# Low parts of stored weights made by an accumulating transfer instead of a VectorE subtraction

## The chip, the cores and the metric

The kernel runs on one core of a Trainium2 chip. The metric is the time of one execution on the device in microseconds (us); the kernel before was timed three times, and beside these stands one profiled execution whose trace is read below. A few names: TensorE (PE in the profile) multiplies matrices, and PEld is its loading of weights; VectorE (DVE), ScalarE (ACT) and GpSimd (POOL) are the other engines; SyncE (SP) issues transfers (DMA). SPq and POOLq are the queues from which SP and POOL issue them.

## The reference, cut to what matters

The reference is one step of a decoder trunk of two layers over 1,024 prompt positions and 8 sample positions (model width 1,024), in float32:

```
p = x @ w_in                        # layer 0: 3072 columns (HGRN2 recurrence + Conformer convolution), layer 1: 3 * 1024 (short conv)
m = mixer(p) @ w_out                # recurrence, depthwise convolution, gates in between
x = layernorm(ALPHA * x + m)
x = layernorm(ALPHA * x + (silu(x @ w1) * (x @ w3)) @ w2)     # hidden width 2816, in both layers
```

What matters here is that every `@` above multiplies by a weight matrix that lies in HBM (memory), and that the results are wanted at nearly float32 precision.

## The kernel before, in words

All activations are kept transposed: 128 features on the partitions, positions along the row. The 1,032 positions form three chunks, `CH`: 0 and 1 of 384 columns and 2 of 264 columns.

**High and low parts.** TensorE multiplies in fp32r, a format with fewer bits than float32. Each operand is therefore split: the high part is the operand rounded to fp32r (`SC.copy`, the CAST on ScalarE at L120), the low part is the operand minus its high part (`VE.tensor_tensor(..., ALU.subtract)` on VectorE at L121). A product takes three matmuls for each 128 rows of weights: low weight by high activation, high by low, high by high (L141, L142, L143). The first of the three needs the weight's low part.

**Units.** A unit is a block of 1,024 x 128 weights (`load_unit`): SP loads 512 KB to a buffer `raw` (R_BUFS = 4 of them), ScalarE makes `wh` of it, VectorE makes `wl` of `raw` and `wh`. `wh` and `wl` have W_BUFS = 3 buffers each, so the split of unit j + 3 can begin only when TensorE has finished with unit j. `mm` runs a unit against one chunk: 8 x 3 matmuls of 384 or 264 columns. In `down` (products by w2) one unit holds several shorter blocks, but again 1,024 x 128 weights in all; sixteen units of `ffn_down` hold half as many.

**Seven products.** `main_g` runs most of the channel mixer for chunks 0 and 1 by a scheme of seven products for a 2 x 2 block product. `project` takes two units of w1 or w3 (`a`, `b`), makes four tiles of split weights and runs seven products of 12 matmuls on them: A11 and A12 (parts of the first unit as it lies in memory), S2 and S3, S4 and S1 (sums and differences of weights, which VectorE forms in `sa` and `sb` first), and A22 (half of the second unit as it lies in memory). Between the w1 and the w3 projection of a pair of blocks stands one `down` of the pair before, two units.

**Order.** The program is written once; a scheduler fixes the order of instructions on each engine when it is built, and every engine then runs its own list in order, waiting on semaphores. The stages on TensorE, in order of time: layer 0's mixer with its convolution interleaved with the first part of its channel mixer (to about 520 us), the rest of its mixer and the head of the channel mixer (to 925), the seven products (to 1163), the 264-column chunk and the norms (to 1259); then layer 1 likewise (mixer to 1532, head to 1785, seven products to 2203, the 264-column chunk and the last norms to the end). In the 264-column stages a unit is used for one chunk only.

Of the kernel before, what the change touches and what calls it, by code (L numbers as in the profile page):

```python
# [19 lines left out]
AF = mybir.ActivationFunctionType  # L20
ALU = mybir.AluOpType
PSUM = bass.MemoryType.PSUM

P = 128
# [5 lines left out]
NK = D // P  # L30
# [38 lines left out]
def trunk(ctx: ExitStack, tc: tile.TileContext, xT, win0, wout0, win1, wout1, w1, w3, w2, vecs, sh, scf, ssc,  # L69
          masks, eye, yT, hp, cp_o, sp_o, hs, cs_o, ss_o):  # L70
    nc = tc.nc
    VE, SC, GP, PE = nc.vector, nc.scalar, nc.gpsimd, nc.tensor
# [46 lines left out]
    def split(hi, lo, src):  # L119
        SC.copy(hi, src)  # L120
        VE.tensor_tensor(lo, src, hi.bitcast(F32), ALU.subtract)  # L121

    def load_unit(src, kt, n=NK):

        wh = wsp.tile([P, NK, P], F32R, name="wh")
        wl = wsp.tile([P, NK, P], F32R, name="wl")
        raw = wsp.tile([P, NK * P], F32, name="raw", bufs=R_BUFS).rearrange("p (k f) -> p k f", f=P)
        src = src.rearrange("p (k f) -> p k f", f=P)
        for k in range(0, kt, n):
            e = min(k + n, kt)  # L130
            nc.sync.dma_start(raw[:, k:e], src[:, k:e])
            split(wh[:, k:e], wl[:, k:e], raw[:, k:e])
        return wh, wl, kt

    def mm(unit, c, parts=None):

        wh, wl, kt = unit
        ps = mmp.tile([P, 512], F32, name="mm")[:, :CH[c][1] - CH[c][0]]
        for k in range(kt):
            h, l = (parts or xp)(k, c)  # L140
            PE.matmul(ps, wl[:, k, :], h, start=k == 0, stop=False)  # L141
            PE.matmul(ps, wh[:, k, :], l, start=False, stop=False)  # L142
            PE.matmul(ps, wh[:, k, :], h, start=False, stop=k == kt - 1)  # L143
        return ps
# [7 lines left out]
    first_x = load_x(0, 2)  # L152
    next(first_x)
    first_unit = [load_unit(win0[4], NK, 4)]
    for _ in first_x:
        pass
# [104 lines left out]
    def residual(m, c, ps, first):  # L261
        v = rc[c][:, m, :]
        if first:
            VE.scalar_tensor_tensor(v, v, ALPHA, ps, ALU.mult, ALU.add)
        else:
            VE.tensor_tensor(v, v, ps, ALU.add)  # L266

    def out_proj(wsrc, chunks):

        for m in range(NK):  # L270
            u = load_unit(wsrc[m], NK)
            for c in chunks:
                residual(m, c, mm(u, c), True)

    def ffn_up(tile_of, l, m, chunks, put, table=True):

        sl = {}
        u = load_unit(w1[l, m], NK)
        for c in chunks:
            s = tile_of(CH[c][1] - CH[c][0])  # L280
            ps = mm(u, c)
            if table:
                SC.activation(s, ps, AF.Silu)
            else:
                SC.activation(s, ps, AF.Sigmoid)
                VE.tensor_tensor(s, ps, s, ALU.mult)
            sl[c] = s
        u = load_unit(w3[l, m], NK)
        for c in chunks:
            s = sl[c]  # L290
            VE.tensor_tensor(s, mm(u, c), s, ALU.mult)
            split(*put(m, c), s)
# [299 lines left out]
    class Swiglu:  # L592
# [10 lines left out]
        def down(self, ms, chunks, first=()):  # L603

            n = len(ms)
            q = NK // n
            for m0 in range(0, NK, q):
                raw = wsp.tile([P, NK * P], F32, name="raw", bufs=R_BUFS).rearrange("p (k f) -> p k f", f=P)
                wh = wsp.tile([P, NK, P], F32R, name="wh")
                wl = wsp.tile([P, NK, P], F32R, name="wl")  # L610
                src = w2[self.l, m0:m0 + q][:, :, ms[0] * P:(ms[0] + n) * P].rearrange("q p f -> p q f")
                nc.sync.dma_start(raw.rearrange("p (q n) f -> p q (n f)", q=q), src)
                split(wh, wl, raw)
                for j in range(q):
                    u = wh[:, j * n:(j + 1) * n], wl[:, j * n:(j + 1) * n], n
                    for c in chunks:
                        residual(m0 + j, c, mm(u, c, lambda k, c: self.parts[ms[k], c]), c in first)
# [53 lines left out]
        def project(self, src, m, out, done):  # L671

            raws = []
            for w in (src[self.l, m], src[self.l, m + 1], None, None):
                r = wsp.tile([P, NK * P], F32, name="raw", bufs=R_BUFS).rearrange("p (k f) -> p k f", f=P)
                if w is not None:
                    nc.sync.dma_start(r, w.rearrange("p (k f) -> p k f", f=P))
                raws.append(r)
            a, b, sa, sb = raws
            lo, hi = slice(0, 4), slice(4, 8)  # L680

            def parts(r, n=NK):
                wh = wsp.tile([P, NK, P], F32R, name="wh")
                wl = wsp.tile([P, NK, P], F32R, name="wl")
                split(wh[:, :n], wl[:, :n], r)
                return [(wh[:, s], wl[:, s]) for s in (lo, hi)]

            def product(w, t):
                ps = mmp.tile([P, 512], F32, name="mm")[:, :384]
                for k in range(4):  # L690
                    PE.matmul(ps, w[1][:, k], t[0][:, k], start=k == 0, stop=False)  # L691
                    PE.matmul(ps, w[0][:, k], t[1][:, k], start=False, stop=False)  # L692
                    PE.matmul(ps, w[0][:, k], t[0][:, k], start=False, stop=k == 3)  # L693
                return ps

            def put(i, c, x, y, op):
                o = out(i, c)
                VE.tensor_tensor(o, x, y, op)
                done(i, c, o)

            A11, A12 = parts(a)
            u, v = self.short(), self.short()
            p1 = product(A11, (X0HA, X0LA))
            SC.copy(u, p1)
            p2 = product(A12, (X0HB, X0LB))
            put(0, 0, u, p2, ALU.add)
            VE.tensor_tensor(sa[:, hi], a[:, lo], b[:, lo], ALU.add)
            VE.tensor_tensor(sa[:, lo], sa[:, hi], b[:, hi], ALU.add)
            S2, S3 = parts(sa)
            p6 = product(S2, self.T2)  # L710
            VE.tensor_tensor(u, u, p6, ALU.add)
            p7 = product(S3, self.T3)
            VE.tensor_tensor(v, p7, u, ALU.subtract)
            VE.tensor_tensor(sb[:, lo], sa[:, lo], a[:, hi], ALU.add)
            VE.tensor_tensor(sb[:, hi], b[:, lo], b[:, hi], ALU.add)
            S4, S1 = parts(sb)
            p3 = product(S4, (X1HB, X1LB))
            VE.tensor_tensor(u, u, p3, ALU.add)
            p5 = product(S1, (X1HA, X1LA))
            put(1, 1, v, p5, ALU.subtract)  # L720
            put(0, 1, u, p5, ALU.add)
            A22, _ = parts(b[:, hi], 4)
            p4 = product(A22, self.T4)
            put(1, 0, v, p4, ALU.add)

# [39 lines left out]
    with tc.tile_pool(name="t0", bufs=1, reuse_waits="tile") as tp:  # L765
        F0.T2, F0.T3 = t_pair(tp, 2), t_pair(tp, 3)
        with tc.tile_pool(name="head0", bufs=1, reuse_waits="tile") as act:
# [6 lines left out]
            for m in range(0, NEARLY, 4):  # L774
# [4 lines left out]
                p = tc.cur_priority  # L779
                F0.down(ms, (1, 2))  # L780
        with tc.tile_pool(name="main0", bufs=1, reuse_waits="tile") as act:
            F0.T4 = t_pair(act, 4)
            F0.main_pool(act)
            q = tc.cur_priority
# [71 lines left out]
    with tc.tile_pool(name="t1", bufs=1, reuse_waits="tile") as tp:  # L856
        F1.T2, F1.T3 = t_pair(tp, 2), t_pair(tp, 3)
        with tc.tile_pool(name="head1", bufs=1, reuse_waits="tile") as act:
# [10 lines left out]
            p = tc.cur_priority  # L869
            F1.down(ms, ALL, ALL)  # L870
        with tc.tile_pool(name="main1", bufs=1, reuse_waits="tile") as act:
            F1.T4 = t_pair(act, 4)
            F1.main_pool(act)
            q = tc.cur_priority
# [74 lines left out]
```

## Time and profile before

| What | Value |
|---|---|
| Time, median of three runs | 2383.87 us (2382.72 to 2384.26) |
| Profiled execution, its own time | 2385.06 us |
| Span of the trace | 2383.2 us |
| Mean granted clock of TensorE | 0.989 of full speed |
| PE busy | 2333.2 us, 98% of the span |
| DVE busy | 1701.4 us, 71% |
| ACT busy | 874.2 us, 37% |
| POOL busy | 45.3 us, 2% |
| Transfers | 229.79 MB, mean 96 GB/s |

Busy time is time in which an engine has at least one instruction under way. The trace's span begins a little after the timed execution does and ends before it, so the profiled time is 1.9 us longer than the span. A busy share near 100% says that an engine is never without work, not that it works at its peak.

### The profile page before, as it was taken

The numbers are of one execution on the slowest core, as the hardware profiler recorded it, in microseconds if no ns is written. First come the engines' busy times: TensorE is split into PE (matmuls) and PEld (weight loads), VectorE is DVE, ScalarE is ACT, GpSimd is POOL, SyncE is SP. The second block draws the span as 40 slices with busy tenths as digits, with TensorE's granted clock in tenths as the row PEclk, the third lists the DMA queues.
The fourth block names the chain that finished last, engine by engine and source line by source line (L and its number), as shares of the span: only waits on it lengthen the run. The fifth ranks groups of instructions, "written<-read, shape, count | busy, mean of one in ns | idle before, by whom it ended". The sixth has DMA issues, their size and how long they took to land.

```text
span 2383.2 us, 36586 instructions
## 1 busy us (share of the span) xinstructions
PE 2333.2 (98%) x14974; PEld 2293.0 (96%) x14974; DVE 1701.4 (71%) x2943; ACT 874.2 (37%) x1479; POOL 45.3 (2%) x40
## 2 busy tenths in 40 slices
PE   9999999999899999999998999999999999999997
PEld 8999899999899999999998999999999999999997
DVE  8998789897863336777686423667957777777775
ACT  5434353335631223332354211435513332332553
POOL 0000000000000000000000000000000000000000
PEclk9999999999999999999999999999999999999998
DMA  5322222453341221222342311334402222132663
GB/s 186 116 78 73 88 78 77 123 167 113 116 131 45 79 73 48 68 80 71 119 149 88 90 53 45 90 115 142 133 27 71 63 80 68 57 89 80 194 196 98
DMA packets 85560, 229.79 MB, mean 96 GB/s; under 512 B 8225, under 2 KB 26401, under 8 KB 85137
## 3 DMA queue, kind: packets, MB, share of 16 engines
q1 hardware_dynamic: 85232, 227.02, 30.9%
q8 instruction: 117, 1.92, 0.3%
q0 software_dynamic: 160, 0.45, 0.1%
q14 instruction: 51, 0.41, 0.1%
HBM read 220.22 MB, written 7.21 MB: 95 GB/s over the span
## 4 chain that ended last, share of the span: by engine, by line
PE 91%; DVE 4%; ACT 2%; POOL 1%; DMA 1%; issue 1%; SPq 0%; POOLq 0%; DVEq 0%; ACTq 0%
PE mm L141 23%; PE mm L142 23%; PE mm L143 23%; PE mm L692 6%; PE mm L693 6%; PE mm L691 6%; PE sm L335 2%; DVE wl L121 1%; POOL rs L194 1%; PE sm L239 1%; DVE r L216 1%; DVE acc L225 1%; ACT r L254 0%; PE sm L382 0%; ACT wh L120 0%
## 5 line engine op out<-in xcount | busy, mean ns | idle before, releaser
L120 ACT CAST wh<-raw 128x1024 fp32r<-128x1024 f32 (+1 forms) x466 | 468.6, 1007 | 899.4 <-PE mm L143 607.5
L121 DVE TENSOR_TENSOR wl<-raw,wh 128x1024 fp32r<-128x1024 f32 (+1 forms) x466 | 544.1, 1169 | 230.4 <-ACT wh L120 226.5
L141 PE MATMUL mm<-x2h,wl 128*128 128x264 f32 x1216 | 349.7, 288 | 7.0 <-DVE wl L121 6.9
L143 PE MATMUL mm<-x2h,wh 128*128 128x264 f32 x1216 | 346.8, 285 | 0.0
L142 PE MATMUL mm<-x2l,wh 128*128 128x264 f32 x1216 | 346.3, 285 | 0.0
L266 DVE TENSOR_TENSOR r<-r,mm 128x384 f32<-128x384 f32 (+1 forms) x336 | 171.5, 521 | 99.6 <-PE mm L143 99.2
L141 PEld LDWEIGHTS mm<-x2h,wl 128*128 128x128 f32 x1216 | 229.8, 189 | 9.6 <-DVE wl L121 8.3
L142 PEld LDWEIGHTS mm<-x2l,wh 128*128 128x128 f32 x1216 | 230.0, 189 | 1.6 <-issue 0.8
L143 PEld LDWEIGHTS mm<-x2h,wh 128*128 128x128 f32 x1216 | 229.1, 188 | 0.1
L141 PE MATMUL mm<-hb,wl 128*128 128x384 f32 (+1 forms) x672 | 211.4, 320 | 8.4 <-ACT hb L120 4.8
L142 PE MATMUL mm<-hb,wh 128*128 128x384 f32 (+1 forms) x672 | 213.1, 319 | 0.0
L143 PE MATMUL mm<-hb,wh 128*128 128x384 f32 (+1 forms) x672 | 212.8, 318 | 0.0
L482 DVE SCALAR_TENSOR_TENSOR cc<-r,vec,cc 128x256 f32<-128x256 f32 (+17 forms) x360 | 189.7, 561 | 0.9
L141 PEld LDWEIGHTS mm<-hb,wl 128*128 128x128 f32 x672 | 125.9, 190 | 10.7 <-ACT hb L120 7.0
L141 PE MATMUL mm<-x0ha,wl 128*128 128x384 f32 x384 | 132.7, 346 | 1.9 <-DVE wl L121 1.9
L143 PE MATMUL mm<-x0ha,wh 128*128 128x384 f32 x384 | 133.2, 347 | 0.0
L142 PE MATMUL mm<-x0la,wh 128*128 128x384 f32 x384 | 132.3, 345 | 0.8 <-DVE x0la L121 0.8
L143 PE MATMUL mm<-x0hb,wh 128*128 128x384 f32 x384 | 132.0, 344 | 0.0
L141 PE MATMUL mm<-x0hb,wl 128*128 128x384 f32 x384 | 131.3, 342 | 0.0
L142 PE MATMUL mm<-x0lb,wh 128*128 128x384 f32 x384 | 131.0, 341 | 0.0
L143 PE MATMUL mm<-x1hb,wh 128*128 128x384 f32 x384 | 130.8, 341 | 0.0
L142 PE MATMUL mm<-x1lb,wh 128*128 128x384 f32 x384 | 130.5, 340 | 0.0
(310 smaller groups left out, 5242.8 us busy)
## 6 DMA issues: line engine op xcount, KB each, us to landing
raw<-in_w SPq DMA_DIRECT2D x256, 512.0 KB, 3.7
raw<-in_win SPq DMA_DIRECT2D x88, 512.0 KB, 3.7
raw<-in_wout SPq DMA_DIRECT2D x48, 512.0 KB, 3.6
raw<-in_w SPq DMA_DIRECT2D x16, 256.0 KB, 2.7
out_yT<-r SPq DMA_DIRECT2D x8, 384.0 KB, 3.4
S0t<-in_sh SPq DMA_DIRECT2D x8, 256.0 KB, 3.2
out_hs<-S0t SPq DMA_DIRECT2D x8, 256.0 KB, 2.0
r<-in_xT SPq DMA_DIRECT2D x4, 384.0 KB, 7.5
```

What stands on the lines that cost most here:

```text
L120: SC.copy(hi, src)
L121: VE.tensor_tensor(lo, src, hi.bitcast(F32), ALU.subtract)
L141: PE.matmul(ps, wl[:, k, :], h, start=k == 0, stop=False)
L142: PE.matmul(ps, wh[:, k, :], l, start=False, stop=False)
L143: PE.matmul(ps, wh[:, k, :], h, start=False, stop=k == kt - 1)
L194: GP.tensor_tensor(dst, dst, mhalf[:p, :n], ALU.pow)
L266: VE.tensor_tensor(v, v, ps, ALU.add)
L335: PE.matmul(ps[:sr, c * 64:(c + 1) * 64].rearrange("p (b i) -> p b i", i=hh), kp[:, c * P:c * P + sr], qr, start=True, stop=True)
L482: VE.scalar_tensor_tensor(acc[:, lo:W], u[:, 30 + lo - d:30 + W - d], col(V_DW + (30 - d) * 4 + i), acc[:, lo:W], ALU.mult, ALU.add)
L691: PE.matmul(ps, w[1][:, k], t[0][:, k], start=k == 0, stop=False)
L692: PE.matmul(ps, w[0][:, k], t[1][:, k], start=False, stop=False)
L693: PE.matmul(ps, w[0][:, k], t[0][:, k], start=False, stop=k == 3)
```

## The change

Weights that lie in memory get their low part in another way. ScalarE writes the negated high part to `wl` (an ACTIVATE that multiplies by -1 and rounds to fp32r), and then a transfer issued by GpSimd reads the same weights from memory a second time and adds them, on the way, to what lies in `wl`. VectorE's subtraction goes for these 409 tiles (410 instructions; 364 of them on 512 KB, the others on half as much). It stays for the sums of weights (S2 to S1 in `project`, 56 tiles) and for all activations.

```diff
+    def split_w(hi, lo, raw, src):
+
+        SC.copy(hi, raw)
+        SC.activation(lo, raw, AF.Copy, scale=-1.0)
+        nc.gpsimd.dma_start(lo, src, accum_op=ALU.add)
+
     def load_unit(src, kt, n=NK):
...
             nc.sync.dma_start(raw[:, k:e], src[:, k:e])
-            split(wh[:, k:e], wl[:, k:e], raw[:, k:e])
+            split_w(wh[:, k:e], wl[:, k:e], raw[:, k:e], src[:, k:e])
...
                 nc.sync.dma_start(raw.rearrange("p (q n) f -> p q (n f)", q=q), src)
-                split(wh, wl, raw)
+                SC.copy(wh, raw)
+                SC.activation(wl, raw, AF.Copy, scale=-1.0)
+                nc.gpsimd.dma_start(wl.rearrange("p (q n) f -> p q (n f)", q=q), src, accum_op=ALU.add)
...
-            def parts(r, n=NK):
+            def parts(r, n=NK, w=None):
                 wh = wsp.tile([P, NK, P], F32R, name="wh")
                 wl = wsp.tile([P, NK, P], F32R, name="wl")
-                split(wh[:, :n], wl[:, :n], r)
+                if w is None:
+                    split(wh[:, :n], wl[:, :n], r)
+                else:
+                    split_w(wh[:, :n], wl[:, :n], r, w.rearrange("p (k f) -> p k f", f=P)[:, NK - n:])
...
-            A11, A12 = parts(a)
+            A11, A12 = parts(a, w=src[self.l, m])
...
-            A22, _ = parts(b[:, hi], 4)
+            A22, _ = parts(b[:, hi], 4, src[self.l, m + 1])
```

Two places of the order that the scheduler makes, before and changed. First GpSimd at the start of the program (`vec`, `ident` and `mraw` are small constants that it loads; the two CASTs make masks of them; the rows at L194 or L200 are the power -0.5 of a norm). Before:

```order
L158 DMA vec<-in_vecs 128x229
L160 DMA ident<-in_eye 128x128
L164 DMA mraw<-in_masks 128x512
L175 CAST mkd<-ident 128x384
L173 CAST mk<-mraw 128x1344
L194 ISA
L194 TENSOR_TENSOR hrs<-hrs,mhalf 128x3 x5
```

Changed:

```order
L164 DMA vec<-in_vecs 128x229
L166 DMA ident<-in_eye 128x128
L170 DMA mraw<-in_masks 128x512
L181 CAST mkd<-ident 128x384
L179 CAST mk<-mraw 128x1344
L127 DMA wl<-in_win 128x512 x2
L127 DMA wl<-in_win 128x1024 x7
L200 ISA
L200 TENSOR_TENSOR hrs<-hrs,mhalf 128x3
```

The accumulating transfers are GpSimd's now, in its one list: the first of them stands behind the two CASTs, and later ones stand ahead of and behind the powers.

Second ScalarE in the last 264-column stage, down to the last unit of the program (`hb` are tiles of the channel mixer, the rows with 128x264 their activations and casts; the rows with 128x1024 are the weights). Before:

```order
L120 CAST wh<-raw 128x1024 x4
L283 ACTIVATE hb<-mm 128x264
L120 CAST wh<-raw 128x1024 x2
L120 CAST hb<-hb 128x264
L283 ACTIVATE hb<-mm 128x264
L120 CAST wh<-raw 128x1024
L120 CAST hb<-hb 128x264
```

Changed:

```order
L126 ACTIVATE wl<-raw 128x1024
L125 CAST wh<-raw 128x1024
L126 ACTIVATE wl<-raw 128x1024
L289 ACTIVATE hb<-mm 128x264
L125 CAST wh<-raw 128x1024
L620 ACTIVATE wl<-raw 128x1024
L120 CAST hb<-hb 128x264
L619 CAST wh<-raw 128x1024
L620 ACTIVATE wl<-raw 128x1024
L289 ACTIVATE hb<-mm 128x264
L619 CAST wh<-raw 128x1024
L120 CAST hb<-hb 128x264
```

Each unit now has two rows on ScalarE, and the negation of a unit (L126, L620) stands ahead of the unit's cast (L125, L619). The order of the matmuls by units on TensorE is the same in both.

## Rows read from the trace of the kernel before

**Rows 1.** The page: busy time of each engine, then its chain of work.

```profile
PE 2333.2 (98%) x14974; PEld 2293.0 (96%) x14974; DVE 1701.4 (71%) x2943; ACT 874.2 (37%) x1479; POOL 45.3 (2%) x40
...
PE 91%; DVE 4%; ACT 2%; POOL 1%; DMA 1%; issue 1%; SPq 0%; POOLq 0%; DVEq 0%; ACTq 0%
```

**Rows 2.** The waits of PE: for whom, us in total, times, longest.

```profile
PE sm L239 <- POOL rs L194: 15.6, 15, 2.1
PE mm L141 <- DVE wl L121: 8.9, 7, 3.6
```

**Rows 3.** The waits of all engines, longest first.

```profile
ACT wh L120 <- PE mm L143: 607.5, 169, 10.4
...
ACT wh L120 <- PE mm L693: 182.4, 84, 3.1
```

**Rows 4.** The groups of instructions by form: count, busy us, mean ns, idle before.

```profile
L121 DVE TENSOR_TENSOR wl<-raw,wh 128x1024 fp32r<-128x1024 f32 x420 | 512.2, 1221 | 229.1 <-ACT wh L120 226.5
L120 ACT CAST wh<-raw 128x1024 fp32r<-128x1024 f32 x420 | 440.1, 1049 | 841.5 <-PE mm L143 589.8 <-PE mm L693 146.8 <-issue 98.5
```

**Rows 5.** The timeline of one unit in the last 264-column stage: start, us, instruction.

```profile
2319.94 0.28 PE L141 MATMUL mm<-x2h,wl 128*128 128x264 f32 x1
...
2320.13 0.39 ACT L283 ACTIVATE hb<-mm 128x264 f32<-128x264 f32 x1 [1.54 <-PE mm L143]
...
2320.42 1.04 ACT L120 CAST wh<-raw 128x1024 fp32r<-128x1024 f32 x1
...
2321.49 1.23 DVE L121 TENSOR_TENSOR wl<-raw,wh 128x1024 fp32r<-128x1024 f32 x1 [1.61 <-ACT wh L120]
...
2322.84 0.28 PE L141 MATMUL mm<-x2h,wl 128*128 128x264 f32 x1
```

**Rows 6.** The timeline of the seven products: S4 begins, later the `down` unit.

```profile
1914.28 0.33 PE L691 MATMUL mm<-x1hb,wl 128*128 128x384 f32 x1
...
1914.52 1.05 ACT L120 CAST wh<-raw 128x1024 fp32r<-128x1024 f32 x1 [2.87 <-PE mm L693]
...
1920.52 0.33 PE L141 MATMUL mm<-hb,wl 128*128 128x384 f32 x1
```

**Rows 7.** The timeline of a 384-column unit, and the next unit's first matmul.

```profile
900.28 0.33 PE L141 MATMUL mm<-x1ha,wl 128*128 128x384 f32 x1
...
904.47 0.28 PE L141 MATMUL mm<-x2h,wl 128*128 128x264 f32 x1
```

**Rows 8.** DMA issues: what, queue, count, KB each, median us from issue to landing.

```profile
raw<-in_w SPq DMA_DIRECT2D x256, 512.0 KB, 3.7
...
vec<-in_vecs POOLq DMA_DIRECT2D x1, 114.5 KB, 4.9
```

**Rows 9.** The page: SP's queue, packets, MB, share of 16 engines' span.

```profile
q1 hardware_dynamic: 85232, 227.02, 30.9%
```

**Rows 10.** Windows by stage: us, busy of PE, PEld, DVE, ACT, POOL (instructions), PE clock, DMA share, GB/s.

```profile
1785.00:2203.00 418.00, 416.93 (x2415) 416.61 (x2414) 319.68 (x510) 132.26 (x184) 0.00 (x0) 1.00 0.24 72
2203.00:2383.00 180.00, 165.38 (x1332) 162.17 (x1330) 124.21 (x180) 82.88 (x117) 4.76 (x3) 0.96 0.52 164
```

**Rows 11.** The timeline of the start: GpSimd, and the first matmuls of units 1 and 2.

```profile
1.25 0.71 POOL L158 DMA_DIRECT2D vec<-in_vecs  x1 [0.81 <-POOLq L925]
1.97 0.54 POOL L160 DMA_DIRECT2D ident<-in_eye  x1
...
8.83 0.45 PE L141 MATMUL mm<-x0ha,wl 128*128 128x384 f32 x1 [1.50 <-DVE wl L121]
9.79 1.69 POOL L173 CAST mk<-mraw 128x1344 uint8<-128x1344 f32 x1 [0.65 <-DMA mraw<-in_masks]
...
15.09 0.44 PE L141 MATMUL mm<-x0ha,wl 128*128 128x384 f32 x1 [0.44 <-DVE wl L121]
```

## Prediction, made before the changed kernel ran

> **What bounds the kernel now.** I read the page first: TensorE has work in 98% of the span and makes up 91% of the chain of work [rows 1]. Then the waits of PE: on low parts of weights it waits 8.9 us in all, on the powers of the norms 15.6 us [rows 2]; with its total idle time of 50 us (2383.2 - 2333.2) that is the most that any change to the other engines can give. Then the waits of all engines: the longest of ScalarE's are its casts of weights waiting for matmuls, 607.5 and 182.4 us [rows 3]. So the splits are early: a cast starts when TensorE gives a buffer back, and then the new tile has time until TensorE comes round to it. I call that time the window. In a 264-column stage a unit takes 2.90 us (2319.94 to 2322.84 [rows 5]); with three buffers the window is two units, 5.80 us. A 384-column unit takes 4.19 us [rows 7], its window is 8.38 us. In the seven products the first `down` unit and the first tile of a w1 projection take the buffer that S2 and S3 leave and are needed after S4, S1 and A22: 1914.28 to 1920.52, a window of 6.24 us [rows 6]. Units used for two or three chunks have 14 us and more. Today a tile needs 0.24 us until the cast starts [rows 6], 1.05 for the cast and 1.22 for the subtraction [rows 4], about 2.6 us with the handover (1.04 from 2320.42, then VectorE at 2321.49 [rows 5]): the narrowest window that matters leaves 3 us over.
>
> **The change, part by part.** The sum is made against the profiled execution, 2385.06 us, which is 1.2 us over the median of the three runs.
>
> *VectorE's subtractions.* 410 go, 364 of them at 1.22 us [rows 4], some 470 us of VectorE's 1701. VectorE is not what TensorE waits for, so I count only the waits that can end sooner: the 8.9 us on low parts, which the new path replaces by its own, and about half of the 15.6 us at norms [rows 2], where fewer subtractions stand between VectorE's steps. Together -17 us, with 0 and -25 as ends.
>
> *ScalarE's negations.* 410 more, priced as the cast of the same shape, 1.05 us [rows 4]: some 405 us, 874 to about 1280 us or 54%. In a 264-column stage a unit then asks 2 x 1.05 us and half of an activation (0.39 us [rows 5]) and of a cast of `hb` of the same size: 2.5 us of 2.90. It fits, so nothing on the path. The order puts the negation ahead of the unit's own cast, so the cast lies beside the transfer and only one of the two is in the chain.
>
> *The transfer: its latency.* The trace has no accumulating transfer. The low end is SP's load of the same 512 KB, 3.7 us from issue to landing; GpSimd's own load `vec` took 4.9 us for 114.5 KB [rows 8]. SP moved 227.02 MB in 30.9% of the span [rows 9], 736 us, or 308 GB/s: 1.70 us for a unit and 0.37 us for `vec`. So a transfer of GpSimd's has about 4.5 us around its bytes, and with a unit's bytes 6.2 us; if the bytes that lie in `wl` have to be read as well, 7.9 us. I take 6.2, since `vec` is the one row with GpSimd as issuer, and keep 3.7 and 7.9. The chain from a free buffer to a usable tile is then 0.24 + 1.05 + 6.2 = 7.5 us (5.0 to 9.2).
>
> *264-column stages, by latency.* Three buffers go round once in the chain plus one unit: a unit takes (7.5 + 2.90) / 3 = 3.47 us, 2.90 at the low end, 4.03 at the high one.
>
> *264-column stages, by bytes.* A unit's load takes 1.70 us of all transfer engines, and the last stage already runs at a share of 0.52 [rows 10]. The accumulating transfer adds 1.70 us if it costs what a load costs, and 3.40 if the bytes in `wl` are a second read: 3.40 or 5.10 us a unit, both over 2.90. I take 4.2 us, between these two and at the high end of the latency. [...]
>
> There are 126 such units (8 + 6 of layer 0's output projection and head, 30 of its channel mixer, 9 of layer 1's mixer, 8 + 6, 54, and 5 in the first stage); 15 of them follow longer units and have windows over 7 us. 111 x (4.2 - 2.90) = **144 us**, with 0 and 244 as ends.
>
> *Seven products.* 14 pairs of blocks, two narrow windows each: 28 x (7.5 - 6.24) = **35 us**, 0 to 28 x 2.96 = 83.
>
> *384-column units for one chunk.* The chain of 7.5 fits into 8.38 us: 0. At 5.1 us of transfers a unit, some 65 of them would lose 0.9 us: 58 as the end.
>
> *Start.* GpSimd's list has the transfers behind its two CASTs, the second of which ends at 11.48 (9.79 + 1.69 [rows 11]). The first half unit lands 4.5 + 0.85 us later, at 16.8; unit 1 then runs 4.19 us without today's gaps and unit 2 begins at 21.0 and not at 15.09 [rows 11]: **+6 us** (3 to 8).
>
> *GpSimd's list.* A power now waits behind the issue of a transfer, 0.54 to 0.71 us [rows 11], which itself waits for a negation; behind the power stand VectorE's multiplication and TensorE. At nine norms that is about +5 us (0 to 20). The issues themselves are 410 x 0.6 = 250 us of an idle engine.
>
> Sum: -17 + 144 + 35 + 6 + 5 = 173; 2385 + 173 = 2558 us for a profiled execution, **2557 us** on the scale of the median.
>
> **Rivals.** *The transfer is covered.* If the chain stays under 5.80 us, that is, if a transfer of GpSimd's lands within 4.5 us, latency costs nothing, and if engines move both streams at once better than [rows 9] says, neither do bytes. Then only the start (+3) and VectorE's relief (-17) are left: 2370 us, faster. For it speaks SP's 3.7 us, against it `vec` with 4.9 us for a fifth of the bytes [rows 8] and the share of 0.52 [rows 10]. The skill's "DMA: Bandwidth & Descriptors" (Anatomy of one DMA) gives 2.0 us plus the bytes at 436 GB/s for a GpSimd transfer, an estimate of 3.2 us here, which would be this rival; `vec` does not agree with it.
>
> *Latency alone.* The accumulating transfer costs what a load costs: a unit takes 3.47 us, 111 x 0.57 = 63, with the other terms +92: 2476 us; with a landing 0.9 us sooner about 2440.
>
> *The accumulating transfer is slow.* At three loads' time, 5.1 us, a unit takes 6.8 us of the transfer engines: 111 x 3.9 = 433, 65 x 2.6 = 169 in the 384-column units, and in the seven products 28 x (0.24 + 1.05 + 4.5 + 5.1 - 6.24) = 130. With the start: some 3110 us. Nothing in the trace excludes it.
>
> *TensorE's clock falls.* The stage with gaps (14.6 us idle of 180) has a granted clock of 0.96, the one without 1.00 [rows 10]. If gaps of 1.3 us in every 4.2 let it fall to 1.2 GHz in the 264-column stages, a unit takes 5.8 us: 111 x 2.9 = 322, about 2735 us.
>
> **How the numbers follow.** The forecast (bytes and latency both, 2480 to 2650): 0.47. Latency alone (2400 to 2480): 0.23. Slow transfer (2700 and up, mostly over 2800): 0.12. Clock (2650 to 2800): 0.08. Covered: 0.10. The time is that of the likeliest, 2557. The range 2400 to 2800 leaves out the covered case and most of the slow one. A measurement of this kernel tells about 0.2% (5 us) from no change. Faster 0.08 (covered); same 0.04 (covered but for the start and norms, or latency alone at its lowest); slower 0.88.
>
> **What would show it.** VectorE about 1230 us busy, ScalarE about 1280. PE's waits at the first matmul of a unit (L147 in the changed code) on a transfer to `wl`, 150 us and more in all, most of them in the four stretches of 264 columns and, singly, at the first `down` unit of a pair; none in stages with units for two or three chunks. A landing of `wl` transfers of about 6 us where the queue is free and more in the last stage, with a DMA share near 1 there; the first matmul of a unit at 16 to 17 us. I am wrong if transfers to `wl` land within 4.5 us (faster), if the DMA share in the last stage stays at 0.8 or less while PE waits (latency, not bytes), or if units of 384 columns wait as well (transfers far slower than two reads).

## The result, and the profile after

The changed kernel takes 2715.9 us (median of 4 runs, 2704.29 to 2724.96) beside 2383.3 us for the kernel before on the same chip: a ratio of 1.139, 95% interval 1.134 to 1.144. It is slower by some 332 us; 2557 was forecast, in a range of 2400 to 2800. The profiled execution took 2721.93 us, its span is 2720.2 us and TensorE's mean granted clock 0.956.

Lines of the profile page of the changed kernel: busy time, transfer queues, two of the costliest groups, and the issues with the median us to landing. They answer to [rows 1], [rows 4], [rows 8] and [rows 9].

```profile
PE 2425.0 (89%) x14974; PEld 2353.6 (87%) x14974; DVE 1280.3 (47%) x2533; ACT 1234.2 (45%) x1889; POOL 412.0 (15%) x450
...
q0 software_dynamic: 76608, 203.37, 43.4%
q1 hardware_dynamic: 85232, 227.02, 25.5%
...
L126 ACT ACTIVATE wl<-raw 128x1024 fp32r<-128x1024 f32 (+1 forms) x338 | 337.8, 1000 | 665.8 <-PE mm L147 520.9
...
L127 POOL DMA_DIRECT2D wl<-in_w x200 | 171.4, 857 | 1121.1 <-ACT wl L126 704.7
...
raw<-in_w SPq DMA_DIRECT2D x256, 512.0 KB, 6.3
wl<-in_w POOLq DMA_DIRECT2D x228, 512.0 KB, 7.4
...
wl<-in_win POOLq DMA_DIRECT2D x88, 512.0 KB, 7.2
...
wl<-in_wout POOLq DMA_DIRECT2D x48, 512.0 KB, 8.1
```

The waits of PE in the changed kernel: us in total, times, longest.

```profile
PE mm L147 <- DMA wl<-in_w: 143.5, 73, 10.0
PE mm L147 <- DMA wl<-in_wout: 53.0, 18, 9.9
PE mm L147 <- DMA wl<-in_win: 34.1, 14, 11.4
PE mm L702 <- DMA wl<-in_w: 11.7, 12, 1.9
PE sm L245 <- POOL rs L200: 6.9, 11, 1.6
```

The span grew by 337.0 us. PE's idle time grew by 245 of them (2720.2 - 2425.0 = 295.2, against 50.0 before), and the four waits on transfers to `wl` make up 242.3. PE's busy time grew by 92 us for the same 14974 matmuls. That is the clock: it fell short of full speed by 0.044 x 2720.2 = 120 us, before by 0.011 x 2383.2 = 26, which is 94 more. VectorE is busy 421 us less, but TensorE had hardly waited for it [rows 2].

Timeline of the last 264-column stage, changed kernel: start, us, instruction.

```profile
2653.18 0.28 PE L147 MATMUL mm<-x2h,wl 128*128 128x264 f32 x1
...
2653.50 1.06 ACT L620 ACTIVATE wl<-raw 128x1024 fp32r<-128x1024 f32 x1 [0.62 <-PE mm L147]
...
2653.55 0.35 PE L147 MATMUL mm<-x2h,wl 128*128 128x264 f32 x1
...
2654.86 1.20 POOL L621 DMA_DIRECT2D wl<-in_w  x1 [1.95 <-ACT hb L120]
...
2658.09 0.39 PE L147 MATMUL mm<-x2h,wl 128*128 128x264 f32 x1 [1.40 <-DMA wl<-in_w]
...
2663.23 0.36 PE L147 MATMUL mm<-hb,wl 128*128 128x264 f32 x1 [1.96 <-DMA wl<-in_w]
```

The chain from a free buffer to a usable low part can be read here link by link. A unit's last matmul on its low part ends at 2653.46 and frees the buffer; the negation starts 0.04 us later and takes 1.06; GpSimd issues the transfer at 2654.86; the low part is there at 2663.2, 8.3 us after the issue. Meanwhile TensorE ran two units, from 2653.55 and 2658.09, of 4.54 and 5.14 us with their waits, where a unit took 2.90 before [rows 5]. The chain takes 9.8 us and the two units without waits would have lasted 5.8.

Windows by stage of the changed kernel: us, busy of PE, PEld, DVE, ACT, POOL, PE clock, DMA share, GB/s. The first is one of 384-column units, the second one of units for several chunks, the third a 264-column stage, the fourth has few loads, and the last two are the last 264-column stage.

```profile
570.00:763.00 193.00, 155.44 (x910) 149.66 (x911) 94.34 (x161) 112.75 (x164) 33.20 (x38) 0.90 0.83 197
763.00:1021.00 258.00, 253.06 (x1678) 252.47 (x1677) 54.55 (x105) 91.04 (x120) 34.76 (x36) 0.99 0.64 140
1275.00:1418.00 143.00, 103.58 (x734) 98.61 (x733) 50.98 (x90) 83.20 (x114) 29.57 (x30) 0.90 0.89 211
...
1958.00:2023.00 65.00, 65.00 (x415) 65.00 (x414) 23.70 (x40) 13.85 (x18) 4.42 (x4) 1.00 0.36 78
2466.00:2577.00 111.00, 85.46 (x614) 81.47 (x613) 37.82 (x64) 63.17 (x81) 25.24 (x27) 0.91 0.99 246
2577.00:2712.00 135.00, 100.33 (x718) 95.60 (x716) 25.70 (x60) 64.27 (x83) 27.30 (x28) 0.91 0.89 209
```

Where TensorE idles (193 - 155 us in the first, 111 - 85 in the fifth) the transfer engines are busy at 0.8 to 1 and the clock is granted at 0.90 or 0.91; where it hardly idles, they are busy at 0.36 to 0.64 and the clock is granted at 0.99 or 1.00. The DMA share of the last stage was 0.52 before [rows 10].

The order of matmuls by units is the same in both kernels, so I paired them one to one and compared, for each pair of neighbours, the times from one start to the next:

| Class of units | Forecast, us | Ahead of a unit's first matmul | Inside units | Measured, us |
|---|---|---|---|---|
| 264 columns, 126 units | 144 | 147 | 19 | 166 |
| 384 columns, one chunk, 122 units | 0 | 77 | 25 | 103 |
| Seven products | 35 | 38 | 3 | 41 |
| Several chunks, 76 units | 0 | 10 | 9 | 19 |
| Start | 6 | | | 8 |

They add up to 337 (the forecast's -17 and +5 for VectorE and GpSimd belong to no single class). The waits are few and long: 117 of them make up the 242 us, and only 70 of the 126 units of 264 columns and 33 of the 122 of 384 columns wait over 0.3 us longer at their first matmul than before.

### The profile page after: what moved, and what is told of

Read it like the earlier page. It is cut to its first block, busy times and chain, and to the rows that moved or that the text cites. A ratio compares the mean times of both kernels' runs of the same rounds, so it can differ in the third digit from the quotient of the medians.

```text
span 2720.2 us, 37747 instructions
## 1 busy us (share of the span) xinstructions
PE 2425.0 (89%) x14974; PEld 2353.6 (87%) x14974; DVE 1280.3 (47%) x2533; ACT 1234.2 (45%) x1889; POOL 412.0 (15%) x450
## 3 DMA queue, kind: packets, MB, share of 16 engines
q0 software_dynamic: 76608, 203.37, 43.4%
q1 hardware_dynamic: 85232, 227.02, 25.5%
HBM read 423.12 MB, written 7.21 MB: 158 GB/s over the span
## 5 line engine op out<-in xcount | busy, mean ns | idle before, releaser
L126 ACT ACTIVATE wl<-raw 128x1024 fp32r<-128x1024 f32 (+1 forms) x338 | 337.8, 1000 | 665.8 <-PE mm L147 520.9
L147 PE MATMUL mm<-x2h,wl 128*128 128x264 f32 x1216 | 365.1, 300 | 108.1 <-DMA wl<-in_w 66.8
L127 POOL DMA_DIRECT2D wl<-in_w x200 | 171.4, 857 | 1121.1 <-ACT wl L126 704.7
L125 ACT CAST wh<-raw 128x1024 fp32r<-128x1024 f32 (+1 forms) x338 | 330.7, 979 | 4.4 <-DMA raw<-in_win 2.3
L488 DVE SCALAR_TENSOR_TENSOR cc<-r,vec,cc 128x384 f32<-128x384 f32 (+15 forms) x360 | 191.2, 562 | 2.5
L147 PE MATMUL mm<-x1ha,wl 128*128 128x384 f32 x384 | 136.7, 356 | 48.4 <-DMA wl<-in_wout 23.3
L120 ACT CAST wh<-raw 128x1024 fp32r<-128x1024 f32 x56 | 58.8, 1051 | 238.7 <-PE mm L149 170.9
L127 POOL DMA_DIRECT2D wl<-in_win x90 | 77.3, 862 | 513.0 <-ACT wl L126 270.4
L620 ACT ACTIVATE wl<-raw 128x1024 fp32r<-128x1024 f32 x72 | 76.3, 1059 | 161.8 <-PE mm L147 68.3
L149 PE MATMUL mm<-x1ha,wh 128*128 128x384 f32 x384 | 135.4, 353 | 0.0
```

Source lines behind the costliest of these rows:

```text
L125: SC.copy(hi, raw)
L126: SC.activation(lo, raw, AF.Copy, scale=-1.0)
L127: nc.gpsimd.dma_start(lo, src, accum_op=ALU.add)
L488: VE.scalar_tensor_tensor(acc[:, lo:W], u[:, 30 + lo - d:30 + W - d], col(V_DW + (30 - d) * 4 + i), acc[:, lo:W], ALU.mult, ALU.add)
L620: SC.activation(wl, raw, AF.Copy, scale=-1.0)
```

## The experiments

The theory: the chain from a free buffer to a landed transfer is longer than the window (latency), and the adding transfer costs the transfer engines two reads (bytes). The rivals were one of the two alone, and ScalarE's second pass. All runs in one table; each stands beside the kernel before on the same chip (2385.23, 2383.78 or 2383.57 us).

| Run | Median, us | Ratio to before, 95% |
|---|---|---|
| Plain transfer in place of the adding one | 2488.2 | 1.043 (1.041 to 1.045) |
| Negation alone | 2399.7 | 1.006 (1.005 to 1.008) |
| Control with smaller buffers | 2726.1 | 1.143 (1.140 to 1.146) |
| Control with four `wl` | 2557.6 | 1.072 (1.070 to 1.075) |
| Transfers on wide units only | 2411.3 | 1.013 (1.011 to 1.015) |
| Low part used last | 2610.6 | 1.095 (1.092 to 1.099) |
| Low part last, four `wl` | 2513.5 | 1.054 (1.052 to 1.057) |
| Adding from `raw` | 2601.1 | 1.091 (1.089 to 1.093) |
| Negation alone on wide units | 2383.8 | 1.000 (0.998 to 1.001) |
| Kernel before, every tile loaded twice | 2440.4 | 1.022 (1.019 to 1.025) |

**Plain transfer.** The same bytes and the same waits, without the adding.

```diff
-        nc.gpsimd.dma_start(lo, src, accum_op=ALU.add)
+        nc.gpsimd.dma_start(lo, src)
```

> As changed, but the transfers of GpSimd copy the weights to wl instead of adding them (so the low parts are the whole weights; work and waits are as in the changed kernel). If the second read of an adding transfer is what costs (packets of 4096 B take 0.33 us there and 0.16 to 0.17 us in SP's loads), a unit costs 1.6 + 1.6 = 3.2 us of the transfer engines instead of 1.6 + 3.0 = 4.6: 264-column units lose 0.3 to 0.5 us each, 384-column units nothing, 2440 to 2480 us, GpSimd's landing about 5.5 to 6 us. If the cost is that GpSimd issues them at all (descriptors, its queue), the time stays near 2690 to 2720 us.

2488.2 us, a little above the 2440 to 2480 of the first case, and the landing came sooner than the 5.5 to 6 us expected. From its profile page, queues and issues:

```profile
q0 software_dynamic: 76608, 203.37, 29.0%
q1 hardware_dynamic: 85232, 227.02, 26.0%
...
wl<-in_w POOLq DMA_DIRECT2D x228, 512.0 KB, 4.3
```

The transfers to `wl` took 29.0% of 2489.2 us, 722 us for 203.37 MB; the adding ones took 43.4% of 2720.2, 1181 us. So adding costs 1.6 times the engines' time, and landing 7.4 and not 4.3 us. A transfer is moved in packets, whose times the trace holds, and these sums include what packets wait for each other. The median packet of 4,096 bytes takes 0.33 us in the adding transfers, 0.17 in the plain ones of the same queue and 0.16 in SP's loads here, so the adding itself costs 1.9 times a plain packet. Plain transfers still cost 103 us over before, so two thirds of the loss (some 230 us) hang on the adding and a third on the rest.

**Negation alone.** ScalarE negates, VectorE adds, there is no transfer.

```diff
-        nc.gpsimd.dma_start(lo, src, accum_op=ALU.add)
+        VE.tensor_tensor(lo, lo.bitcast(F32), raw, ALU.add)
```

> ScalarE negates as in the changed kernel, but VectorE adds the weights to the negated high part; no transfer of GpSimd's. If ScalarE's 410 more instructions are off the path, as the forecast had it: 2378 to 2395 us. If they are on it (ScalarE is in one list with activations that the matmuls wait for): 2420 us and more.

2399.7 us, 14.5 over before and above the range expected. PE waits for VectorE's low parts nearly twice as long as before [rows 2]:

```profile
PE mm L147 <- DVE wl L127: 16.3, 9, 5.4
```

ScalarE's second pass isn't free, but small beside 332.

**Four buffers.** Two runs: a control with smaller pools elsewhere, which makes room, and the same with a fourth `wl` buffer (`wh` keeps three).

```diff
-SL_BUFS = 6
+SL_BUFS = 3
-HB_BUFS = 18
-TP_BUFS = 4
+HB_BUFS = 17
+TP_BUFS = 3
...
-        wl = wsp.tile([P, NK, P], F32R, name="wl")
+        wl = wsp.tile([P, NK, P], F32R, name="wl", bufs=W_BUFS + 1)
```

> The changed kernel with smaller pools elsewhere (SL_BUFS 3, TP_BUFS 3, HB_BUFS 17, 256 bytes less for descriptors), which make room for a fourth wl buffer in the next kernel. It serves as that kernel's base: 2700 to 2760 us.

> As the control, with four wl buffers instead of three: the window of a 264-column unit grows from 5.8 to 8.7 us, of a 384-column unit from 8.4 to 12.6. If the chain from free buffer to landed transfer (about 8.7 us) is the bound, both kinds of units fit: 200 us and more under the control, about 2480 us. If the bytes are the bound (4.6 us of transfer engines a unit against 2.90 and 4.19 us of matmuls), the 264-column stages stay at about 4.6 us a unit and a share of 0.9 and more: 20 to 80 us under the control.

The control took 2726.1 us, the fourth buffer 168.5 us less, which lies between the two ranges and nearer to that of latency. The transfers are the same and landed no sooner (7.9 us for `in_w`), so this part of the loss was latency: time that a longer window covers. Bytes alone fell here as a theory. The narrow windows of the seven products lost nothing any more, the 384-column units 59 us in place of 103, the 264-column units 95 in place of 166. What is left, 172 us over before, doesn't refute latency alone yet: a chain of 0.24 + 1.05 + 7.9 = 9.2 us is longer than three units of 2.90, too.

**Low part last.** The window is stretched in another way: the matmuls on the high part of all eight rows of a unit run first.

```diff
-            PE.matmul(ps, wl[:, k, :], h, start=k == 0, stop=False)
-            PE.matmul(ps, wh[:, k, :], l, start=False, stop=False)
-            PE.matmul(ps, wh[:, k, :], h, start=False, stop=k == kt - 1)
+            PE.matmul(ps, wh[:, k, :], l, start=k == 0, stop=False)
+            PE.matmul(ps, wh[:, k, :], h, start=False, stop=False)
+        for k in range(kt):
+            h, l = (parts or xp)(k, c)
+            PE.matmul(ps, wl[:, k, :], h, start=False, stop=k == kt - 1)
```

> The changed kernel with the matmuls of a product in another order: first high by low and high by high for all blocks, then low by high for all. The low part is needed 16 matmuls later: the window grows by 1.9 us in a 264-column unit (to 7.7), by 2.8 in a 384-column unit (to 11.2), by 1.4 in the seven products (to 7.6). If latency is about half of the loss, as four wl buffers say (168 us back): 384-column units and seven products come back, 264-column units in part, 2570 to 2630 us. If only bytes counted: 2690 us and more.

> Both, the later low part and four wl buffers (with the control's smaller pools): windows of 10.6 us and more everywhere, over the landing. What is left is bytes: 8 packets of 0.16 and 8 of 0.33 us for each engine and unit are 3.9 us, against 2.90 us of matmuls: 126 units x 1.0 = 126 us at most, and the later start of 8 us: 2480 to 2530 us, with a DMA share near 1 in the last stage. If it falls under 2430, bytes are no bound either.

2610.6 and, with four buffers, 2513.5 us, both in the range that was expected. Waits of PE and windows of the last stage in the second of them:

```profile
PE mm L151 <- DMA wl<-in_w: 54.4, 37, 7.2
PE mm L147 <- DVE hb L121: 19.3, 11, 4.3
PE mm L151 <- DMA wl<-in_wout: 10.2, 6, 4.1
...
PE mm L151 <- DMA wl<-in_win: 6.5, 6, 2.5
```

```profile
2288.00:2386.00 98.00, 83.97 (x615) 79.88 (x614) 32.37 (x56) 63.29 (x80) 25.20 (x26) 0.93 1.06 273
2386.00:2510.00 124.00, 99.98 (x720) 94.93 (x718) 30.85 (x68) 63.95 (x82) 26.83 (x27) 0.90 0.91 226
```

The stage takes 222 us in place of 246, with the same DMA share. So a share near 1 alone did not prove that bytes set the pace in the changed kernel: a packet's time in the trace holds its waiting for others too. In this last run bytes are a likely bound all the same: at the median time of each kind of packet, those of the two windows ask 209 of the 222 us of all transfer engines. This is an estimate from the trace, and no run sets bytes apart. The 19.3 us on `hb` are waits for activations that the new order of matmuls brought.

**Adding from `raw`.** The transfer reads the copy of the weights that SP has already brought to the chip.

```diff
-        nc.gpsimd.dma_start(lo, src, accum_op=ALU.add)
+        nc.gpsimd.dma_start(lo, raw, accum_op=ALU.add)
```

> As changed, but the transfer reads the weights from raw (on the chip) and not a second time from memory: 203 MB less read from memory, the same number of reads by the transfer engines, and raw is held until the transfer has landed. If the memory is what slows it, packets fall to 0.17 us and the time to 2500; if it is the two reads of the transfer engines, packets of 4096 B still take 0.33 us, and the time stays at 2650 to 2780 us.

2601.1 us, in neither of the two ranges. From its profile page:

```profile
q0 software_dynamic: 59200, 203.37, 42.3%
...
HBM read 220.22 MB, written 7.21 MB: 87 GB/s over the span
...
wl<-raw POOLq DMA_DIRECT2D x364, 512.0 KB, 5.8
```

Memory is read half as much (423.12 MB in the changed kernel) and the transfer lands 1.6 us sooner, and 115 us come back. The engines' time hardly changes: 42.3% of 2601.0 is 1100 us, against 1181, and the median packet of 4,096 bytes takes 0.34 us, against 0.33. So the price of adding lies in the transfer itself, not in the second read of memory.

**Every tile loaded twice.** The split of before, but SP loads each tile twice into the same buffer: a second plain read, meant to cost bytes and to stay out of the chain.

```diff
             nc.sync.dma_start(raw[:, k:e], src[:, k:e])
+            nc.sync.dma_start(raw[:, k:e], src[:, k:e])
```

> The split of the kernel before, but SP loads every weight tile twice into the same buffer, so that a second plain read of all weights is there, in the prefetched stream and not in the chain from a free buffer to a usable low part. If the bytes of a second read cost by themselves, a 264-column unit takes two loads at 1.60 to 1.70 us, 3.2 to 3.4 us against 2.90: 126 x 0.3 to 0.5 = 38 to 63 us, so 2420 to 2450 us. If the plain transfer's loss of 103 us was latency alone, this takes 2384 to 2395 us.

2440.4 us, 57 over before and in the range that bytes gave. Its queue and issues, then waits of SP, of ScalarE and of PE:

```profile
q1 hardware_dynamic: 161680, 437.28, 55.8%
...
raw<-in_w SPq DMA_DIRECT2D x512, 512.0 KB, 4.4
```

```profile
SPq L132 <- DMA raw<-in_w: 277.3, 130, 6.4
...
ACT wh L120 <- DMA raw<-in_w: 101.8, 54, 6.2
...
PE mm L142 <- DVE wl L121: 41.0, 25, 5.0
```

The run does not do what it was meant to. The second load (L132) writes the buffer that the first one fills, and SP waits until the first has landed: in all 410 pairs the second is issued after that. A `raw` buffer is full 9.0 us (median) after its first issue, where one load took 3.7 [rows 8], and ScalarE's casts now wait for it. So this run made a chain longer too, its 57 us can't be put down to bytes, and latency alone is not refuted by it. By the pairing 40 us lie in the 264-column units.

**Wide units only.** The transfer is kept for the units that serve two or three chunks, which I took to have 14 us and more (76 of them by the trace, not 74); then the same with VectorE adding in place of the transfer.

```diff
-            split_w(wh[:, k:e], wl[:, k:e], raw[:, k:e], src[:, k:e])
+            if wide:
+                split_w(wh[:, k:e], wl[:, k:e], raw[:, k:e], src[:, k:e])
+            else:
+                split(wh[:, k:e], wl[:, k:e], raw[:, k:e])
...
-            u = load_unit(wsrc[m], NK)
+            u = load_unit(wsrc[m], NK, wide=len(chunks) > 1)
```

> The accumulating transfer for 74 units alone, those used for two or three chunks with windows of 14 us and more; all other units split as before. If what counts is whether chain and bytes fit into the window, nothing waits: within 5 us of the kernel before (2379 to 2389), no gain worth the name, since VectorE was not waited for. If accumulating transfers harm by themselves (GpSimd's list, contention with loads): 2400 us and more.

> The 74 units with windows of 14 us and more have their high part negated by ScalarE, and VectorE adds the weights to it; no unit has an accumulating transfer, all other units are split as before. This is the run on wide windows without its transfers. If the 27 us lost there come from the transfers (traffic beside SP's loads, GpSimd's list ahead of the powers), this takes 2381 to 2391 us. If they come from ScalarE's second pass ahead of its other work, it takes 2400 us and more, and the transfers were innocent there.

With the transfers 2411.3 us, without them 2383.8: they alone cost 27 us, though all of them should have been covered. PE's waits, and the longest of them in the timeline, in the run with transfers:

```profile
PE mm L150 <- DMA wl<-in_win: 7.8, 2, 4.3
...
PE mm L150 <- DMA wl<-in_w: 5.6, 2, 3.1
```

```profile
1361.28 0.69 PE L150 MATMUL mm<-x0ha,wl 128*128 128x384 f32 x1 [4.25 <-DMA wl<-in_win]
```

All four waits stand at the first matmul of a wide unit that follows units for one chunk, in three cases of 264 columns. A unit's window is set by the two units ahead of it, not by its own length; I had read it off the unit itself. These are 13.4 us. The other half was not traced to a place. No version with the transfer was faster than the kernel before.

## Why the prediction was right and wrong

*Right: the direction, and where the waits stand.* TensorE waits for transfers to `wl` at a unit's first matmul, for 242 us (150 and more were named), more than half of it in the 264-column stretches, and in the seven products at the two places that the forecast named. VectorE is busy for 1280 us (1230 forecast), ScalarE for 1234 (1280), the first matmul starts at 17.68 (16 to 17).

*The landing was too short.* Forecast 6.2 us (3.7 to 7.9), medians of 7.2 to 8.1 measured. `vec`, from which it was built, was the first in GpSimd's queue. It was not the only row with GpSimd as issuer: two more loads stood behind it in the same trace, and by the same working (0.85 us for its 256 KB and 1.70 for 512 KB at [rows 9]'s 308 GB/s) `mraw` would have given an estimate of 7.2 - 0.85 + 1.70, about 8 us.

```profile
mraw<-in_masks POOLq DMA_DIRECT2D x1, 256.0 KB, 7.2
...
ident<-in_eye POOLq DMA_DIRECT2D x1, 64.0 KB, 6.1
```

The changed kernel's trace shows the same thing: a transfer of 512 KB to `wl` lands in 6.7 us (median) when no other transfer to `wl` is under way at its issue, in 7.5 behind one and in 9.1 behind two. SP's own loads slowed from 3.7 to 6.3 us under the new traffic, and the same transfer without adding landed in 4.0 to 4.7.

*Seven products: 35 forecast, 41 measured.* Timeline of one of the projections in the changed kernel, the two narrow windows (A11's product and the first `down` unit):

```profile
2345.52 0.42 PE L702 MATMUL mm<-x0ha,wl 128*128 128x384 f32 x1 [0.73 <-DMA wl<-in_w]
...
2361.33 0.41 PE L147 MATMUL mm<-hb,wl 128*128 128x384 f32 x1 [0.97 <-DMA wl<-in_w]
```

Waits of 0.7 to 1.0 us behind a window of 6.24 us [rows 6] make a chain of 7.0 to 7.2 here; over all 28 such places the 38 us are 1.36 each, a chain of 7.6, where the forecast had 7.5. In this stage with few loads the landing of 6.2 us was about right; it is the dense stages that lengthened it.

*264-column units: 144 forecast, 166 measured.* The size of 1.30 us a unit holds on average: the 106 units that follow two others of 264 columns lost 138 us ahead of their first matmul, the 20 others 9, and 19 us lie inside the units. That it came out so near is partly luck. The forecast took 4.2 us as a middle between two prices of bytes; the chain of 9.8 us read above gives (9.8 + 2.90) / 3 = 4.23 by latency, where the forecast's chain of 7.5 gave 3.47. So the size doesn't tell latency from bytes. Of the runs, four buffers and the low part last take away 213 of the control's 341 us, which a longer window covers, and the 130 us that stay are the most that bytes can cost in that kernel (the waits on `hb` and ScalarE's second pass are in them too). No run gives a lower end for bytes, so that both are needed, as forecast, is likely from the 209 of 222 us above but not shown.

*384-column units: the step that failed.* "The chain of 7.5 fits into 8.38 us: 0", with 58 as the end; measured 103. With the median landings the chain is 8.5 to 9.4 us and doesn't fit, and four buffers took the 103 down to 59. But by the forecast's own formula such a chain costs (8.5 + 4.19) / 3 to (9.4 + 4.19) / 3, at most 0.34 us a unit or 41 us in all. What a median doesn't show are single late transfers: 33 units wait, by 2.4 us on average and by 9.8 at most, and a landing takes up to 12.0. With the landing of 5.8 us in the run from `raw` (chain 7.1 us) 55 were left, which the median doesn't account for either. The forecast had named waits of these units as a sign that a transfer takes far more than two reads; they waited, and it doesn't (a packet takes 1.9 times a plain one), so the sign was read wrongly.

*Clock: a rival that held in part.* Its figure, 2735, is close, but not by its mechanism, which had the 264-column stages at 1.2 GHz throughout; they were granted 0.90 to 0.91 here, a mean between 1.2 and 2.4 GHz that lies near the higher, after stretches in which PE waited for transfers. Busy time grew by 92 us with it. That is no extra 92 us on top of the table: where the next transfer sets the pace, a slower matmul only shortens the wait. The forecast had no term for it in the sum; that its 2735 is near is luck, and what the clock alone costs stays open.

*The price of adding.* 1181 us for 203.37 MB is 172 GB/s, SP's loads run at 327 (227.02 MB in 694 us): a ratio of 1.9, 3.04 and 1.60 us a unit, as the high end had it (3.40 and 1.70). That this is a second read, of the bytes in `wl`, fits the ratio but was not shown apart from it. "Collectives: The Full Stack" in the Trainium skill (The bandwidth ceiling: the fold count) says of ReduceScatter that it runs at half the rate of AllGather because its add needs two source reads, and limits its model to rings of three ranks and more; there is no ring here, and the measured 1.9 is of the same size. With the high end in the sum, 5.10 us a unit and 244 in place of 144, the time would have been 2657 and nearer to the result, but by luck: the 264-column units lost 166. "DMA: Bandwidth & Descriptors" in the Trainium skill (Anatomy of one DMA) gives 2.0 us plus the bytes at 436 GB/s for a GpSimd transfer, an estimate of 3.2 us for 512 KB; even the plain transfer took 4.0 to 4.7 here, beside other traffic, so the measurement decides against it.

*Priced at nothing.* ScalarE's negations, forecast as covered, cost 14.5 us alone. On the 76 wide units they cost nothing that can be seen (2383.8), but an even share of 14.5 would be 2.7 us there, about what the interval leaves room for, so which units pay is not shown. Units of several chunks were put at 0 and lost 19 us: their window was read off their own length. VectorE's relief (-17) has one visible part: the wait at the norms fell from 15.6 [rows 2] to 6.9 us.

## What to carry to other kernels

Moving work from an engine that nobody waits for to a queue puts the queue's latency into every buffer's round: compare the landing under load (here 7 to 8 us, not the 3.7 of a quiet load) with the window that the units ahead of it leave, and pay for buffers or a later use first. A chain that was forecast to fit by less than a microsecond did not fit here, since the new traffic slowed the transfers that it was measured by; look at late landings too, not at the median alone. Price an adding transfer at about twice a plain one (0.33 to 0.34 us a packet against 0.17 here), wherever its source lies. And before a run is read as one of bytes alone, look in its trace at what each added transfer waits for.

## What the runs showed of the hardware that was not expected

- Adding costs the transfer engines about the same whether the source lies in memory or on the chip: 1181 against 1100 us for 203.37 MB, 0.33 against 0.34 us for the median packet of 4,096 bytes. The landing differs by 1.6 us (7.4 and 5.8).
- A GpSimd issue of such a transfer occupies its engine for 0.86 us on average (171.4 us for the 200 of `in_w` at L127; 1.2 us for those at L621), against 0.54 in the run with plain transfers and 0.54 to 0.71 for small ones before [rows 11].
- An adding transfer lands later the more of its kind are under way: in 6.7, 7.5 and 9.1 us (medians) behind none, one and two others to `wl` in the changed kernel.
- The transfers slow each other: SP's loads land in 3.7 us alone, 4.4 with each tile loaded twice, 4.8 beside plain transfers of GpSimd and 6.3 beside adding ones.
- TensorE's mean granted clock was lower where PE idled more: 0.989 before (50 us idle), 0.981 with the tiles loaded twice (90), 0.974 beside plain transfers (120), 0.956 in the changed kernel (295). It is no strict order: the control idles 302 us at 0.961.
